# State updates of a gated linear attention as three fp32r products instead of one fp32 product

## The chip, the cores and the metric

The kernel runs on one core of a Trainium2 chip. The core has a matrix engine (PE, with its weight loads shown apart as PEld), a vector engine (DVE), a scalar engine (ACT), a third elementwise engine (POOL) and a queue that issues the transfers (SP). Each engine works through its own queue in order; semaphores make one engine wait for another. The metric is the device time of one execution in microseconds (us), the median of several runs. The scratch memory that all engines use is SBUF; PE writes its products to PSUM, from where DVE and ACT read them. POOL doesn't read PSUM here.

## The reference, cut to what matters

```python
h = rmsnorm(x, norm_g)
q, k, v, z_a, lr_f, lr_b, b_gate, c_gate, h_c, z_c = split(h @ w_in)      # 1024 tokens, 4 heads
# per head and direction (forward, and backward on the flipped sequence), in chunks:
#   o     = att(q, k) @ v  +  q_in @ state
#   state = decay * state  +  k_out.T @ v          # the state update: 128 x 256 per head
o = o_fwd + o_bwd
o = o * rsqrt(mean(o * o) + EPS) * gla_norm_g      # over the 256 columns of a head
y = concat([o * silu(z_a), short_conv(...) * silu(z_c)])
out = rmsnorm(x + y @ w_out, final_g)
```

All inputs and outputs are float32.

## The kernel before, in words

Sequence and feature sizes are 1024; tokens go in 8 blocks of 128 (`t`), there are 4 heads (`h`), keys have 128 and values 256 columns. The first 577 us project `x` to `q`, `k`, `v`, the gates and the convolution, with every fp32 operand split in two fp32r parts (`split`, L151: `hi` is a rounded copy, `lo` the rest) and three products for one, `hi*hi`, `hi*lo`, `lo*hi`; the results go to DRAM by head.

The last stage, which the change touches, runs the heads. For each head `load_head` and `load_z` (L703, L722) bring back decays `b`, keys, queries, values and the gate `z`. Ahead of head 0 its backward states are built in 7 steps. Then, for head h and block t (the loop at L923):

- `output` (L814) adds up to three fp32 products in the PSUM tile `po`: backward state, forward state, and `at` times `v` (L824). ACT squares `po` and sums the squares (`osq`, `oss`, L828), `inv_rms` adds eps on DVE (L147) and raises to -1/2 on POOL (L148), ACT scales `po` by that to `on` (L830). `po` has one buffer.
- `turns` (L856) transposes up to two key blocks on PE (`pk`, L861) and copies each to SBUF on ACT (`ks`, L862): the forward key block of this head and the backward one of the next head, whose states are built one head ahead. `states` (L865) multiplies each with its block of `v` in one fp32 product (`pu`, L869), and DVE adds the product to the decayed state (`s0`, `s1`, L876). In heads 0 to 2 there are two such updates in 7 of the 8 blocks, in head 3 one, in the 7 steps ahead of head 0 one.
- `scores` (L802) makes three fp32 products in `pa`; DVE copies the first to `at` (L809) and overwrites it under two masks (L810, L811). `at` is an operand of the next block's `po`.
- `store` (L833) transposes `on` to `py` on PE, and DVE multiplies it with `z` (`yt`, L844).
- `prep_f` and `prep_b` (L764, L754) compute the decayed queries and keys of the blocks ahead: `dd`, `qs`, `qx`, `kx`, `ko`, `e` on DVE and ACT, `kt` times `k` on POOL (L779). These DVE instructions read two SBUF operands.
- `more` (L887) fills PE between these steps with products of the output projection (`out`, L667), whose results DVE adds to `res` (L669).

In this stage the code fixes only what depends on what; a scheduler of the library, with durations of its own, sets the order of each engine's queue when the kernel is built, and puts in the waits. Another set of instructions can so change the order of all others.

Of the kernel before, what the change touches and what calls it, by code (L numbers as in the profile page):

```python
# [9 lines left out]
F32 = mybir.dt.float32  # L10
F32R = mybir.dt.float32r
I32 = mybir.dt.int32
BF16 = mybir.dt.bfloat16
AF = mybir.ActivationFunctionType
ALU = mybir.AluOpType
# [3 lines left out]
P = 128  # L19
S = 1024  # L20
D = 1024
NH = 4
DK = 128
DV = 256
# [3 lines left out]
EPS = 1e-6  # L28
# [9 lines left out]
def tile_hybrid_gla_shortconv(ctx, tc, x, norm_g, w_in, w_gk_f, b_gk_f, w_gk_b, b_gk_b,  # L38
                              gla_norm_g, conv_w, conv_b, w_out, final_g, out):
    nc = tc.nc  # L40
    V, A, G, T = nc.vector, nc.scalar, nc.gpsimd, nc.tensor
# [6 lines left out]
    stat = ctx.enter_context(tc.tile_pool(name="stat", bufs=4))  # L48
# [15 lines left out]
    z_dram = [dram.tile([P, 2, S], F32, name=f"z_dram{h}") for h in range(NH)]  # L64
# [35 lines left out]
    for d, wg in enumerate((w_gk_f, w_gk_b)):  # L100
        for r in range(4):
            o = d * 64 + r * RANK
# [7 lines left out]
    mhalf = const.tile([P, 1], F32, name="mhalf")  # L110
# [33 lines left out]
    def inv_rms(ss, eps_n):  # L144

        rs = stat.tile([P, 1], F32, name="rs", bufs=6)
        V.tensor_scalar(rs, ss, eps_n, None, ALU.add)  # L147
        G.tensor_tensor(rs, rs, mhalf, ALU.pow)  # L148
        return rs

    def split(hi, lo, src, e_hi=A, e_lo=G):  # L151

        (e_hi.copy if e_hi is A else e_hi.tensor_copy)(hi, src)  # L153
        e_lo.tensor_tensor(lo, src, hi.bitcast(F32), ALU.subtract)  # L154
# [14 lines left out]
    def scale_of(t):  # L169
        sq = xp.tile([P, D], BF16, name="sq", bufs=2)  # L170
        ss = stat.tile([P, 1], F32, name="ss")
        A.activation(sq, xts[t], AF.Square, accum_out=ss)
        return inv_rms(ss, D * EPS)
# [59 lines left out]
    with tc.manual_schedule():  # L233
# [24 lines left out]
        for t in range(NT):  # L258
            ps = bank()[:, 0:DV]
            mul_v(ps, t, wv, 0)  # L260
            if t + 2 < NT:
                rs = scale_of(t + 2)
# [24 lines left out]
    for half in range(2):  # L287
        lps = bank()
        for c in range(ND):
            for j in range(2):  # L290
                T.matmul(lps, lrw[:, c, :], hb[c // 4][half][j][:, c % 4, :],  # L291
                         start=c == 0 and j == 0, stop=c == ND - 1 and j == 1)
# [341 lines left out]
    dq = gl.enter_context(tc.tile_pool(name="dq", bufs=2, reuse_waits="tile"))  # L634
    hd = gl.enter_context(tc.tile_pool(name="hd", bufs=2, reuse_waits="tile"))
    hx = gl.enter_context(tc.tile_pool(name="hx", bufs=2, reuse_waits="tile"))
    pg = gl.enter_context(tc.tile_pool(name="pg", bufs=1, space=PSUM, reuse_waits="tile"))
    GS = 2
# [81 lines left out]
        return r  # L720

    def load_z(h, r):  # L722
        for half in range(2):
            z = hx.tile([P, 2, 512], F32, name="z", bufs=3)
            nc.sync.dma_start(z, z_dram[h][:, :, half * 512:half * 512 + 512])
            r["sz"].append(z)

    def decays(r):
# [73 lines left out]
    def scores(r, g, t):  # L802
        i = t % GS
        pa = pg.tile([P, 3, P], F32, name="pa", bufs=2)
        T.matmul(pa[:, 0], fl(r["kx"][:, t]), fl(g["qx"][:, i]), start=True, stop=True)
        T.matmul(pa[:, 1], fl(g["kt"][0][:, i]), fl(g["qt"][0][:, i]), start=True, stop=True)
        T.matmul(pa[:, 2], fl(g["kt"][1][:, i]), fl(g["qt"][1][:, i]), start=True, stop=True)
        at = dq.tile([P, P], F32, name="at")
        V.tensor_copy(at, pa[:, 0])  # L809
        V.copy_predicated(at, mask_f_i, pa[:, 1])  # L810
        V.copy_predicated(at, mask_b_i, pa[:, 2])  # L811
        return at

    def output(r, g, t, at, s_f):  # L814
        i = t % GS
        o = pg.tile([P, DV], F32, name="po")
        mm = []
        if r["sb"][t] is not None:
            mm.append((fl(g["qs"][1][:, i]), r["sb"][t]))
        if s_f is not None:  # L820
            mm.append((fl(g["qs"][0][:, i]), s_f))
        mm.append((at, r["v"][:, t]))
        for j, (l, m) in enumerate(mm):
            T.matmul(o, l, m, start=j == 0, stop=j == len(mm) - 1)  # L824

        sq = dq.tile([P, DV], BF16, name="osq", bufs=1)
        ss = stat.tile([P, 1], F32, name="oss")
        A.activation(sq, o, AF.Square, accum_out=ss)  # L828
        on = dq.tile([P, DV], F32, name="on")
        A.activation(on, o, AF.Copy, scale=inv_rms(ss, DV * EPS * DK))  # L830
        return on

    def store(h, r, py, t, on):  # L833
        i = t % GS
        if i == 0:
            py[0] = pg.tile([P, 2, GS * P], F32, name="py")
        for e2 in range(2):
            T.transpose(py[0][:, e2, i * P:(i + 1) * P], on[:, e2 * P:(e2 + 1) * P], ident)
        if i == GS - 1:
            r0 = t + 1 - GS  # L840
            yt = dq.tile([P, 2, GS * P], F32, name="yt")
            for e2 in range(2):
                o4 = r0 % 4 * P
                V.scalar_tensor_tensor(yt[:, e2], py[0][:, e2], gng_h[:, e2:e2 + 1],  # L844
                                       r["sz"][r0 // 4][:, e2, o4:o4 + GS * P], ALU.mult, ALU.mult)
            if h < NH - 1:
                nc.sync.dma_start(ya_dram[:, h * 2:h * 2 + 2, r0 * P:(r0 + GS) * P], yt)
                return
            for j in range(GS):
                raw = ws.tile([P, 4, P], F32, name="s", bufs=3)  # L850
                nc.sync.dma_start(raw[:, 0:2], ya_dram[:, 2 * h - 2:2 * h, (r0 + j) * P:(r0 + j + 1) * P])
                y = y_last[r0 + j] = y_pair()
                for k, src in ((0, raw[:, 0:2]), (2, yt[:, :, j * P:(j + 1) * P])):
                    split(y[0][:, k:k + 2], y[1][:, k:k + 2], src)

    def turns(items):  # L856

        pk = pg.tile([P, 2, P], F32, name="pk")
        ks = dq.tile([P, 2, P], F32, name="ks")
        for r, t, d, kt in items:  # L860
            T.transpose(pk[:, d], kt, ident)  # L861
            A.copy(ks[:, d], pk[:, d])  # L862
        return ks

    def states(items, ks, s_f):  # L865

        pu = pg.tile([P, 2, DV], F32, name="pu")
        for r, t, d, kt in items:
            T.matmul(pu[:, d], ks[:, d], r["v"][:, t], start=True, stop=True)  # L869
        for r, t, d, kt in items:  # L870
            s = st.tile([P, DV], F32, name=f"s{d}", bufs=(2, NT + 1)[d])
            old = s_f if d == 0 else r["sb"][t]
            if old is None:
                V.tensor_copy(s, pu[:, d])
            else:
                V.scalar_tensor_tensor(s, old, r["dp"][d][:, t:t + 1], pu[:, d], ALU.mult, ALU.add)  # L876
            if d == 0:
                s_f = s
            else:
                r["sb"][t - 1] = s  # L880
        return s_f
# [23 lines left out]
    for t in range(NT - 1, 0, -1):  # L905
        if t % GS == GS - 1:
            ko1[0, t // GS] = prep_b(heads[0], t + 1 - GS)
        items = [(heads[0], t, 1, fl(ko1[0, t // GS][:, t % GS]))]
        ks = turns(items)
        more(3)  # L910
        states(items, ks, None)
        more(3)
        if t == 4:
            load_z(0, heads[0])
    gs = {(0, 0): {}}
    for _ in prep_f(heads[0], 0, gs[0, 0]):
        pass
    at = {(0, 0): scores(heads[0], gs[0, 0], 0)}
    heads.append(start_head(1))
    ons = []  # L920
    py = [None]
    ahead = iter(())
    for h in range(NH):  # L923
        r = heads[h]
        nxt = heads[h + 1] if h + 1 < NH else None
        s_f = None
        if nxt is not None:
            load_z(h + 1, nxt)
        for t in range(NT):
            n = h * NT + t  # L930
# [14 lines left out]
            def step(k=2):  # L945
                more(share.pop(0))
                for _ in range(k):
                    next(ahead, None)
            g = gs[h, t // GS]
            on = output(r, g, t, at[h, t], s_f)  # L950
            step()
            items = []
# [3 lines left out]
            if nxt is not None and tb > 0:  # L956
                items.append((nxt, tb, 1, fl(ko1[h + 1, tb // GS][:, tb % GS])))
            ks = turns(items) if items else None
            if ons:
                store(*ons.pop())  # L960
            step()
            step(0)
            if items:
                s_f = states(items, ks, s_f)
            step(0 if t % 2 == 0 else 4)
            ons.append((h, r, py, t, on))
            if n + 1 < NH * NT:
                hh, tt = divmod(n + 1, NT)
                if t % GS == GS - 1:
                    for _ in ahead:  # L970
                        pass
                at[hh, tt] = scores(heads[hh], gs[hh, tt // GS], tt)
            step(0)
        if h + 2 < NH:
            heads.append(start_head(h + 2))
    store(*ons.pop())
    more(NT * NT)
    gl.close()
# [22 lines left out]
```

## Time and profile before

| | |
|---|---|
| median of 3 runs | 878.18 us (878.04 to 878.6) |
| the profiled execution | 879.14 us, of which the span from first to last instruction is 877.4 |
| PE busy | 859.9 us, 98% of the span |
| DVE, ACT, POOL busy | 644.3, 374.1, 396.2 us |
| last stage, heads and output projection | from about 577 us to the end |
| fp32 products of state updates | 56, two records each |

How it is read: a busy engine is one that has an instruction under way. PE's products overlap, each starts before the one ahead of it has drained, so their cost is the step from one start to the next and not their length. A chain of waits is read from a timeline: what an instruction waited for stands behind it in brackets, with the idle time.

### The profile page before, as it was taken

How to read it: one execution, taken by the hardware profiler on the slowest of the kernel's cores; microseconds unless marked ns; L12 is line 12 of the kernel's file. 1: busy time of each engine (PE TensorE's matmuls, PEld its weight loads, DVE VectorE, ACT ScalarE, POOL GpSimd, SP SyncE). 2: the span in 40 equal slices, each digit the busy share in tenths (PEclk: the TensorE clock that was granted, in tenths of full speed). 3: DMA queues.
4: the chain of work that ended last, by engine and by line, in shares of the span. 5: the costliest groups of instructions: out<-in, count | busy, mean ns of one | idle time of the engine just before them, and what ended most of it. 6: DMA issues, size and time to landing. Idle time of an engine off the chain costs nothing.

```text
span 877.4 us, 12286 instructions
## 1 busy us (share of the span) xinstructions
PE 859.9 (98%) x4236; PEld 713.9 (81%) x4236; DVE 644.3 (73%) x1181; ACT 374.1 (43%) x771; POOL 396.2 (45%) x349
## 2 busy tenths in 40 slices
PE   7999999999999999999999999999999999999996
PEld 6999987878787877878788888887877787878885
DVE  5889738696868787786864445468799989976664
ACT  4633223354434343544532233334464546542553
POOL 3423756667666666767654453601112122221231
PEclk9999999999999999999999999999999999999999
DMA  8511441314222222413153342579575333310122
GB/s 305 117 55 48 123 120 49 96 52 116 58 87 72 72 85 61 121 48 118 44 163 97 98 127 88 174 238 397 166 231 186 121 126 125 110 37 24 43 79 96
DMA packets 102160, 100.30 MB, mean 114 GB/s; under 512 B 10705, under 2 KB 82385, under 8 KB 101586
## 3 DMA queue, kind: packets, MB, share of 16 engines
q1 hardware_dynamic: 102098, 99.53, 36.3%
q8 instruction: 33, 0.54, 0.3%
q14 instruction: 29, 0.24, 0.1%
HBM read 71.20 MB, written 28.31 MB: 113 GB/s over the span
## 4 chain that ended last, share of the span: by engine, by line
PE 90%; DVE 5%; DMA 3%; issue 1%; ACT 1%; SPq 0%; POOLq 0%; POOL 0%; DVEq 0%; ACTq 0%
PE pb L390 18%; PE pc L390 18%; PE pa L390 18%; PE out L667 16%; PE out L223 5%; PE po L824 3%; PE pu L869 2%; PE pc L466 2%; PE pb L466 2%; PE pa L466 1%; PE out L538 1%; DMA b<-b_dram 1%; DMA k<-k_dram 1%; PE out L291 1%; DMA xt<-in_x 1%
## 5 line engine op out<-in xcount | busy, mean ns | idle before, releaser
L154 POOL TENSOR_TENSOR a_lo<-raw,a_hi 128x512 fp32r<-128x512 f32 x84 | 124.7, 1493 | 43.2 <-ACT a_hi L153 38.7
L154 POOL TENSOR_TENSOR a_lo<-tmp,a_hi 128x512 fp32r<-128x512 f32 x48 | 72.4, 1509 | 101.9 <-ACT a_hi L153 100.3
L153 ACT CAST a_hi<-tmp 128x512 fp32r<-128x512 f32 x48 | 29.6, 617 | 156.4 <-DVE tmp L416 127.7
L153 ACT CAST a_hi<-raw 128x512 fp32r<-128x512 f32 x108 | 65.6, 619 | 64.2 <-POOL a_lo L154 21.1
L148 POOL TENSOR_TENSOR rs<-rs,mhalf 128x1 f32<-128x1 f32 x48 | 28.7, 598 | 142.2 <-DVE rs L147 134.8
L667 PE MATMUL out<-a_hi,y_hi 128*128 128x512 f32 x192 | 88.8, 463 | 0.5 <-ACT y_hi L153 0.5
L154 POOL TENSOR_TENSOR a_lo<-s,a_hi 128x512 fp32r<-128x512 f32 x50 | 74.4, 1488 | 18.8 <-ACT a_hi L153 16.4
L667 PE MATMUL out<-a_hi,y_lo 128*128 128x512 f32 x192 | 76.9, 401 | 0.0
L667 PE MATMUL out<-a_lo,y_hi 128*128 128x512 f32 x192 | 76.7, 400 | 0.0
L779 POOL TENSOR_TENSOR kt<-kt,k 128x256 f32<-128x256 f32 x32 | 26.3, 823 | 95.1 <-ACT kt L776 71.8
L416 DVE TENSOR_TENSOR s<-raw 128x512 f32<-128x512 f32 x24 | 29.1, 1214 | 50.2 <-DMA raw<-in_w_in 49.8
L390 PE MATMUL pc<-h_hi,a_lo 128*128 128x512 f32 x128 | 50.4, 394 | 0.0
L390 PE MATMUL pb<-h_hi,a_lo 128*128 128x512 f32 x128 | 50.4, 393 | 0.0
L390 PE MATMUL pa<-h_hi,a_lo 128*128 128x512 f32 x128 | 50.4, 393 | 0.0
L390 PE MATMUL pa<-h_lo,a_hi 128*128 128x512 f32 x128 | 50.2, 393 | 0.0
L390 PE MATMUL pb<-h_lo,a_hi 128*128 128x512 f32 x128 | 50.2, 393 | 0.0
L390 PE MATMUL pc<-h_lo,a_hi 128*128 128x512 f32 x128 | 50.2, 392 | 0.0
L390 PE MATMUL pb<-h_hi,a_hi 128*128 128x512 f32 x128 | 50.1, 392 | 0.0
L390 PE MATMUL pc<-h_hi,a_hi 128*128 128x512 f32 x128 | 50.1, 392 | 0.0
L390 PE MATMUL pa<-h_hi,a_hi 128*128 128x512 f32 x128 | 50.0, 391 | 0.0
L438 DVE TENSOR_TENSOR tmp<-pa,tmp 128x512 f32<-128x512 f32 x48 | 32.5, 685 | 22.7 <-PE pa L390 22.1
L438 DVE TENSOR_TENSOR tmp<-pc,tmp 128x512 f32<-128x512 f32 x48 | 32.5, 686 | 20.0 <-PE pc L390 19.5
(263 smaller groups left out, 2514.1 us busy)
## 6 DMA issues: line engine op xcount, KB each, us to landing
raw<-in_w_in SPq DMA_DIRECT2D x56, 512.0 KB, 4.1
raw<-in_w_out SPq DMA_DIRECT2D x16, 512.0 KB, 4.0
xt<-in_x SPq DMA_DIRECT2D x8, 512.0 KB, 8.4
yc_dram<-tmp SPq DMA_DIRECT2D x16, 256.0 KB, 3.3
b_dram<-u SPq DMA_DIRECT2D x8, 512.0 KB, 2.6
z_dram<-tmp SPq DMA_DIRECT2D x16, 256.0 KB, 2.9
s<-yc_dram SPq DMA_DIRECT2D x16, 256.0 KB, 4.2
raw<-in_x SPq DMA_DIRECT2D x8, 512.0 KB, 6.1
```

Source lines behind the costliest of these rows:

```text
L148: G.tensor_tensor(rs, rs, mhalf, ALU.pow)
L153: (e_hi.copy if e_hi is A else e_hi.tensor_copy)(hi, src)
L154: e_lo.tensor_tensor(lo, src, hi.bitcast(F32), ALU.subtract)
L223: last_mm[0] = T.matmul(ps, h_tile(a, c, t), wv[c // 4][w_][:, c % 4, :], start=part == 0 and c == 0, stop=part == 2 and c == ND - 1)
L390: T.matmul(ps, a[x0][:, k], b_[x1][:, k], start=start and k == 0 and j == 0, stop=stop and k == n - 1 and j == 2, skip_group_check=not start)
L416: V.tensor_tensor(f, x0, x1, op)
L438: step(V.tensor_tensor(f, ps, x, ALU.add))
L466: T.matmul(ps[:, t * DV:(t + 1) * DV], b_[x1][:, k, tok], fl(o[k // 2][x0])[:, k % 2 * DV:k % 2 * DV + DV], start=k == 0 and j == 0, stop= ...
L667: T.matmul(ps, a[:, j, :], w, start=j == 0 and i == 0, stop=j == 3 and i == 2)
L779: G.tensor_tensor(kk, kk, k4, ALU.mult)
L824: T.matmul(o, l, m, start=j == 0, stop=j == len(mm) - 1)
L869: T.matmul(pu[:, d], ks[:, d], r["v"][:, t], start=True, stop=True)
```

## The change

The state update's fp32 product becomes three fp32r products of split parts. `turns` now splits `v` of each update in `vh` (a copy on ACT) and `vl` (a subtraction on POOL), and the key block in `ks` (ACT's copy out of PSUM, now rounded to fp32r) and `kl` (a subtraction on DVE, one instruction over both key blocks of a step). `states` multiplies `ks*vh`, `ks*vl`, `kl*vh`. Three other edits: the first copy of `at` moves from DVE to ACT; `po` becomes one fixed PSUM tile of 257 columns, the last of which holds the square root of the eps term, so that the sum of squares includes eps and `inv_rms` falls away in `output` (POOL's power reads `oss` directly); `z` is loaded in four pieces of 256 columns with five buffers instead of two of 512 with three.

```diff
     def load_z(h, r):
-        for half in range(2):
-            z = hx.tile([P, 2, 512], F32, name="z", bufs=3)
-            nc.sync.dma_start(z, z_dram[h][:, :, half * 512:half * 512 + 512])
+        n = GS * P
+        for i in range(S // n):
+            z = hx.tile([P, 2, n], F32, name="z", bufs=5)
+            nc.sync.dma_start(z, z_dram[h][:, :, i * n:i * n + n])
             r["sz"].append(z)
...
         at = dq.tile([P, P], F32, name="at")
-        V.tensor_copy(at, pa[:, 0])
+        A.copy(at, pa[:, 0])
         V.copy_predicated(at, mask_f_i, pa[:, 1])
...
+    po = pg.tile([P, DV + 1], F32, name="po")
+    V.memset(po[:, DV:DV + 1], (DV * EPS * DK) ** 0.5)
     def output(r, g, t, at, s_f):
-        o = pg.tile([P, DV], F32, name="po")
+        o = po[:, 0:DV]
...
-        A.activation(sq, o, AF.Square, accum_out=ss)
+        A.activation(sq, po, AF.Square, accum_out=ss)
+        rs = stat.tile([P, 1], F32, name="rs", bufs=6)
+        G.tensor_tensor(rs, ss, mhalf, ALU.pow)
         on = dq.tile([P, DV], F32, name="on")
-        A.activation(on, o, AF.Copy, scale=inv_rms(ss, DV * EPS * DK))
+        A.activation(on, o, AF.Copy, scale=rs)
...
     def turns(items):
+        vs = []
+        for r, t, d, kt in items:
+            v = tuple(dq.tile([P, DV], F32R, name=n, bufs=b) for n, b in (("vh", 3), ("vl", 2)))
+            split(*v, r["v"][:, t])
+            vs.append(v)
         pk = pg.tile([P, 2, P], F32, name="pk")
-        ks = dq.tile([P, 2, P], F32, name="ks")
+        ks, kl = (dq.tile([P, 2, P], F32R, name=n) for n in ("ks", "kl"))
         for r, t, d, kt in items:
             T.transpose(pk[:, d], kt, ident)
             A.copy(ks[:, d], pk[:, d])
-        return ks
+        ds = [d for r, t, d, kt in items]
+        both = slice(min(ds), max(ds) + 1)
+        V.tensor_tensor(kl[:, both], pk[:, both], ks[:, both].bitcast(F32), ALU.subtract)
+        return ks, kl, vs
-    def states(items, ks, s_f):
+    def states(items, kv, s_f):
+        kh, kl, vs = kv
         pu = pg.tile([P, 2, DV], F32, name="pu")
-        for r, t, d, kt in items:
-            T.matmul(pu[:, d], ks[:, d], r["v"][:, t], start=True, stop=True)
+        for (r, t, d, kt), (vh, vl) in zip(items, vs):
+            for j, (a, v) in enumerate(((kh, vh), (kh, vl), (kl, vh))):
+                T.matmul(pu[:, d], a[:, d], v, start=j == 0, stop=j == 2)
```

The change also gives the scheduler another set of instructions. Three places of the built programs follow, all in head 1 around the output of its fifth block; numbers in names are buffers of the build, L numbers those of the respective file.

PE before, behind the last product of `po` (its first key transpose stands ahead of that product): one transpose, six projection products, the two updates.

```order
L861 MATMUL pk_6767<-ident_148,ko1_6740 128x128
L667 MATMUL out_6722<-a_hi_6082,y_hi_6718 128x512
L667 MATMUL out_6722<-a_lo_6083,y_hi_6718 128x512
L667 MATMUL out_6722<-a_hi_6082,y_lo_6719 128x512
L667 MATMUL out_6722<-w_hi_6092,y_hi_6718 128x512
L667 MATMUL out_6722<-w_lo_6093,y_hi_6718 128x512
L667 MATMUL out_6722<-w_hi_6092,y_lo_6719 128x512
L869 MATMUL pu_6796<-v_5763,ks_6768 128x256
L869 MATMUL pu_6796<-v_6415,ks_6768 128x256
```

PE now, behind the last product of `po`, up to the first product that reads `kl`:

```order
L873 MATMUL pk_6973<-ident_148,ko0_6897 128x128
L845 MATMUL py_6888<-ident_148,on_6862 128x128 x2
L667 MATMUL out_6922<-a_hi_6196,y_hi_6918 128x512
L667 MATMUL out_6922<-a_lo_6197,y_hi_6918 128x512
L667 MATMUL out_6922<-a_hi_6196,y_lo_6919 128x512
L873 MATMUL pk_6973<-ident_148,ko1_6940 128x128
L667 MATMUL out_6922<-w_hi_6206,y_hi_6918 128x512
L667 MATMUL out_6922<-w_lo_6207,y_hi_6918 128x512
L667 MATMUL out_6922<-w_hi_6206,y_lo_6919 128x512
L886 MATMUL pu_7004<-vh_6965,ks_6974 128x256
L886 MATMUL pu_7004<-vl_6966,ks_6974 128x256
L886 MATMUL pu_7004<-vh_6965,kl_6975 128x256
```

Both key transposes and those of `on` now stand behind `po`, and the second key transpose has three projection products, not six, between it and the updates.

ACT before, at the same place: both key copies stand ahead of `on`.

```order
L862 COPY ks_6768<-pk_6767 128x128
L828 ACTIVATE osq_6748,oss_6749<-po_6744 128x256
L862 COPY ks_6768<-pk_6767 128x128
L830 ACTIVATE on_6751<-po_6744,rs_6752 128x256
L733 ACTIVATE dc0_7037<-b0_7033 128x16
```

ACT now:

```order
L833 ACTIVATE osq_6947,oss_6948<-po_5335 128x257
L874 CAST ks_6974<-pk_6973 128x128
L734 ACTIVATE dc0_7271<-b0_7267 128x16
L837 ACTIVATE on_6952<-po_5335,rs_6950 128x256
L874 CAST ks_6974<-pk_6973 128x128
L153 CAST vh_7052<-v_6563 128x256
L153 CAST vh_7141<-v_5825 128x256
```

The second key copy has moved behind `on`, and the copies of `v` for later blocks have come in behind it.

DVE before, in the same block, from the state updates to the end of `at`:

```order
L876 SCALAR_TENSOR_TENSOR s0_6799<-s0_6712,dp0_5771,pu_6796 128x256
L876 SCALAR_TENSOR_TENSOR s1_6801<-s1_6714,dp1_6427,pu_6796 128x256
L786 TENSOR_TENSOR qx_6908<-q_6419,e_6917 128x2x64
L786 TENSOR_TENSOR qx_6908<-q_6419,e_6983 128x2x64
L809 COPY at_6811<-pa_6807 128x128
L778 TENSOR_TENSOR qt0_6911<-qt0_6911,q_6419 128x256
L810 COPY_PREDICATED at_6811<-mask_f_160,pa_6807 128x128
L772 TENSOR_TENSOR dd_6938<-b1_6411 128x256
L811 COPY_PREDICATED at_6811<-mask_b_161,pa_6807 128x128
```

DVE now:

```order
L893 SCALAR_TENSOR_TENSOR s0_7011<-s0_6912,dp0_5833,pu_7004 128x256
L893 SCALAR_TENSOR_TENSOR s1_7013<-s1_6914,dp1_6575,pu_7004 128x256
L787 TENSOR_TENSOR qx_7130<-q_6567,e_7139 128x2x64
L787 TENSOR_TENSOR qx_7130<-q_6567,e_7217 128x2x64
L779 TENSOR_TENSOR qt0_7133<-qt0_7133,q_6567 128x256
L811 COPY_PREDICATED at_7023<-mask_f_160,pa_7019 128x128
L773 TENSOR_TENSOR dd_7170<-b1_6559 128x256
L812 COPY_PREDICATED at_7023<-mask_b_161,pa_7019 128x128
```

The copy is gone from this queue and the rest stands as it stood.

## Rows read from the trace of the kernel before

**Rows 1.** The page: busy us of each engine, share of span, instructions.
```profile
PE 859.9 (98%) x4236; PEld 713.9 (81%) x4236; DVE 644.3 (73%) x1181; ACT 374.1 (43%) x771; POOL 396.2 (45%) x349
```

**Rows 2.** Stretches of heads 0, 1, 2: length, each engine's busy us (instructions), clock, DMA.
```profile
626.50:675.40 48.90, 47.11 (x243) 38.62 (x242) 46.04 (x143) 28.36 (x84) 11.44 (x16) 1.00 0.58 188
675.40:725.40 50.00, 48.75 (x248) 39.25 (x247) 45.19 (x144) 23.86 (x76) 11.06 (x16) 1.00 0.39 127
725.40:774.90 49.50, 48.68 (x246) 39.39 (x246) 46.70 (x140) 27.56 (x81) 11.85 (x16) 1.00 0.34 104
```

**Rows 3.** Waits, 577 us to the end: who waited for whom, us, times, longest.
```profile
PEld po L824 <- DVE at L811: 9.0, 18, 1.1
...
PE po L824 <- DVE at L811: 3.0, 9, 0.8
```

**Rows 4.** Timeline, fp32 products of 128x256: start, us, engine, line, operands, records.
```profile
705.53 1.03 PE L824 MATMUL po<-s,qs 128*128 128x256 f32 x4
706.39 0.27 PE L861 MATMUL pk<-ident,ko 128*128 128x128 f32 x1
```

**Rows 5.** Timeline of PE in an earlier stage, fp32r products of 128x256, 28 rows.
```profile
83.74 0.28 PE L466 MATMUL pc<-a_hi,t_lo 128*128 128x256 f32 x1
83.86 0.28 PE L466 MATMUL pc<-a_lo,t_hi 128*128 128x256 f32 x1
...
86.92 0.28 PE L466 MATMUL pa<-a_hi,t_lo 128*128 128x256 f32 x1
```

**Rows 6.** DVE's groups from 577 us: busy us, mean ns, idle before, releaser.
```profile
L876 DVE SCALAR_TENSOR_TENSOR s<-s,dp,pu 128x256 f32<-128x256 f32 x48 | 21.3, 474 | 4.5 <-PE pu L869 4.3
L772 DVE TENSOR_TENSOR dd<-b 128x256 f32<-128x256 f32 x32 | 16.0, 502 | 0.1
...
L787 DVE TENSOR_TENSOR qs<-qx,dc 128x128 f32<-128x128 f32 x32 | 12.0, 375 | 0.0
...
L809 DVE COPY at<-pa 128x128 f32<-128x128 f32 x32 | 9.1, 285 | 1.3 <-PE pa L807 1.2
...
L147 DVE TENSOR_SCALAR rs<-oss 128x1 f32<-128x1 f32 x32 | 4.8, 149 | 7.3 <-ACT osq L828 6.8
```

**Rows 7.** Timeline, POOL's product beside DVE; the last row is undisturbed.
```profile
705.66 0.73 POOL L779 TENSOR_TENSOR kt<-kt,k 128x256 f32<-128x256 f32 x1 [3.00 <-ACT kt L776]
705.80 0.88 DVE L772 TENSOR_TENSOR dd<-b 128x256 f32<-128x256 f32 x1
...
706.93 0.70 PE L824 MATMUL po<-v,at 128*128 128x256 f32 x2 [0.27 <-DVE at L811]
...
709.21 0.41 DVE L772 TENSOR_TENSOR dd<-b 128x256 f32<-128x256 f32 x1
```

**Rows 8.** Issues by tile: count, KB each, median us from issue to landing.
```profile
v<-v_dram SPq DMA_DIRECT2D x4, 1024.0 KB, 6.6
z<-z_dram SPq DMA_DIRECT2D x8, 512.0 KB, 5.7
```

**Rows 9.** Timeline, head 1, behind its fifth block's output.
```profile
700.56 0.70 PE L824 MATMUL po<-v,at 128*128 128x256 f32 x2
...
701.58 0.19 ACT L828 ACTIVATION_READ_ACCUMULATOR osq<-po 128x1 f32 x1
...
701.88 0.15 DVE L147 TENSOR_SCALAR rs<-oss 128x1 f32<-128x1 f32 x1 [0.34 <-ACT osq L828]
...
702.11 0.55 POOL L148 TENSOR_TENSOR rs<-rs,mhalf 128x1 f32<-128x1 f32 x1 [5.33 <-DVE rs L147]
...
702.60 1.02 PE L869 MATMUL pu<-v,ks 128*128 128x256 f32 x4
702.69 0.47 ACT L830 ACTIVATE on<-po,rs 128x256 f32<-128x256 f32 x1 [0.76 <-POOL rs L148]
```

**Rows 10.** Timeline, head 2: a key copy behind `on`; POOL beside a state update.
```profile
758.48 0.47 ACT L830 ACTIVATE on<-po,rs 128x256 f32<-128x256 f32 x1 [0.73 <-POOL rs L148]
...
758.85 0.26 ACT L862 COPY ks<-pk 128x128 f32<-128x128 f32 x1
...
759.16 0.70 PE L869 MATMUL pu<-v,ks 128*128 128x256 f32 x2 [0.33 <-ACT ks L862]
...
759.55 0.75 POOL L779 TENSOR_TENSOR kt<-kt,k 128x256 f32<-128x256 f32 x1 [1.11 <-issue]
...
759.90 0.87 DVE L876 SCALAR_TENSOR_TENSOR s<-s,dp,pu 128x256 f32<-128x256 f32 x2 [0.18 <-PE pu L869]
```

More of the change, by code (lines that the diff above doesn't have):

```diff
@@ L824, in output @@
             T.matmul(o, l, m, start=j == 0, stop=j == len(mm) - 1)
-        sq = dq.tile([P, DV], BF16, name="osq", bufs=1)
+        sq = dq.tile([P, DV + 1], BF16, name="osq", bufs=1)
         ss = stat.tile([P, 1], F32, name="oss")
-        A.activation(sq, o, AF.Square, accum_out=ss)
+        A.activation(sq, po, AF.Square, accum_out=ss)
+        rs = stat.tile([P, 1], F32, name="rs", bufs=6)
+        G.tensor_tensor(rs, ss, mhalf, ALU.pow)
         on = dq.tile([P, DV], F32, name="on")
-        A.activation(on, o, AF.Copy, scale=inv_rms(ss, DV * EPS * DK))
+        A.activation(on, o, AF.Copy, scale=rs)
         return on
@@ L842, in store @@
             for e2 in range(2):
-                o4 = r0 % 4 * P
                 V.scalar_tensor_tensor(yt[:, e2], py[0][:, e2], gng_h[:, e2:e2 + 1],
-                                       r["sz"][r0 // 4][:, e2, o4:o4 + GS * P], ALU.mult, ALU.mult)
+                                       r["sz"][r0 // GS][:, e2], ALU.mult, ALU.mult)
             if h < NH - 1:
```

## Prediction

> **What bounds the kernel now.** I read the page first: TensorE is busy 98% of the span [rows 1]; what remains is the stages. The change touches only the last one, from 577 us on, where the four attention heads run between the products of the output projection. By stretch [rows 2], PE is busy 97 to 98% while heads 0, 1 and 2 run (626.5 to 774.9), and DVE is nearly as full there: 137.9 of 148.4 us, 10.5 us left. ACT has half its time free and POOL three quarters. So two engines are close to the bound, PE sets the time, and what PE loses are waits inside a block of 128 tokens (24 blocks in that stretch, 6.2 us each). The list of waits names the largest: the last product of `po` waits for `at`, which DVE finishes: 3.0 us seen as idle PE and 9.0 us seen by the weight load ahead of it [rows 3]. Spacing the products' ends, I put the real loss at some 7.6 us of the stage's 300. The reader should keep two questions apart: how many product slots PE must issue, and which chain ends last ahead of the products that wait.
>
> **Product slots.** Each key block's update is one fp32 product of 128x256, recorded as two instructions. Four such records stand 0.86 us apart from what follows them (705.53 to 706.39) [rows 4], so one product takes 0.43 us. The three new products are fp32r of 128x256: 27 steps from 83.74 to 86.92 [rows 5] make 0.118 us each, 0.353 for three. There are 56 updates (7 ahead of the heads, 7 times 2 in each of heads 0 to 2, 7 in head 3): 56 x (0.43 - 0.353) = **-4.4 us** of PE time. The weights change at each of these rows too, so the price holds for products with new weights.
>
> The Trainium skill (TensorE: Matmul & The Clock Gate, Back-to-back issue gap) gives 256 columns N/2.4 + 2.5 ns, which is 109 ns; the rows above show 118, and the measurement decides. By the page's figure the term would be -5.8 us, an estimate.
>
> **Work beside the products, on DVE.** Per block the copy of `at` (0.285) and the eps addition (0.149) go [rows 6], 32 of each: -13.9. The subtraction for `kl` comes, 21 times over both halves (0.474, as the state update, which also reads 128x256 from PSUM) and 14 times over one (0.285): +13.9. DVE's own load is even. ACT gets 56 copies of `v` (128x256) and 32 of `at`, some 1.1 us per block, into its free half; POOL gets 56 subtractions of 0.73 us (its 128x256 product with `k` [rows 7]), some 1.5 us per block, into its free three quarters. The z loads become four of 256 KB instead of two of 512 KB per head: on SP's queue each waits for the same kind of release as before (an earlier z tile read by DVE), the weights and stores behind it stand a few positions earlier or later, and none of them is among the waits of the trace; I cost it at nothing, and at most at one landing of 5.7 us [rows 8] if a tile were late. The eps column adds one element to a 0.38 us square.
>
> **The new wait ahead of the third product.** Before, the second key copy was all that the second update needed. Now `kl` covers both halves, so the third product needs pk's second transpose, ACT's copy of it and DVE's subtraction. The order (first two fences) shows what is new: in 10 of the 21 blocks with two updates ACT's second key copy stands behind `on`, which waits for POOL's power, which waits for the square of `po`. At the place shown, today [rows 9]: `po` ends at 701.26, the square with its read-out at 701.77, the eps addition hands over at 702.03, POOL starts at 702.11, `on` at 702.69. Without the addition the 0.34 us from 701.77 to 702.11 shrink to about 0.1, so `on` starts at 702.45; the next ACT instruction starts 0.37 later (758.48 to 758.85) [rows 10], the copy takes 0.26, the subtraction 0.47, hand-overs 0.1: `kl` at 703.65, which is 2.4 us behind the end of `po`; 2.7 where an exponential stands between. PE meanwhile issues, at that place, two transposes for pk and two for py (0.11 each), six projection products (0.23, twice the columns of [rows 5]) and two updates' products: 2.05 us, from 701.11 on (702.60 less the 1.49 that lie between today). It arrives at 703.16 and waits 0.5. By the same count the cover is 2.05 at two of the ten places (0.5 each), 2.28 at five (three with an exponential between, 0.57 each, two at 0.26) and 2.51 at three (0.34, and twice nothing): **+3.6 us**. The trace has this pattern once today, and it does cost: the second update waits 0.33 for ACT's copy behind `on` [rows 10]; that place goes, so **+3.3**. Bounds: 0 if PE is late at these places anyway, and +6 if the weight load adds 0.1 to 0.2 at each and DVE's queue ahead of `kl` (up to 2.4 us of work at three of them) ends later than ACT's.
>
> **The wait for `at`.** Three things move. DVE's queue between the state update and the second predicated copy loses the copy, 0.23 us of its time. ACT's copy now comes between, 0.26 and a hand-over, but DVE reaches the predicated copy later than that by the order shown (third pair of fences). And PE arrives earlier at about half the places, by 0.11 to 0.33, because transposes have moved behind `po`. Against this stands what [rows 7] show: while POOL multiplies `kt` (705.66, 0.73 us), DVE's `dd`, two SBUF inputs, takes 0.88 instead of 0.41 (709.21), its end follows POOL's, and `po` waits 0.27 for `at` right behind it. A state update, which reads PSUM, keeps its 0.87 for two beside the same POOL instruction (759.55, 759.90) [rows 10]. The first `vl` of a block runs beside such PSUM work, the second ends about 0.3 us after DVE turned to SBUF work ahead of `at`. I take -0.23 - 0.1 (removed addition) + 0.3 as **0**; bounds -3.8 (half of the 7.6) and +6 (0.3 at 20 places).
>
> The Trainium skill states the same as a rule (SBUF — State Buffer, Who interferes with whom): a DVE instruction with two SBUF inputs and a GpSimd instruction that reads SBUF exclude each other for the whole instruction. The trace agrees for `dd`, 0.88 against 0.41. It speaks against this change, which adds 56 such GpSimd instructions; it is the second rival.
>
> **Sum.** -4.4 + 3.3 + 0 = -1.1 us. On the profiled execution: 879.14 (span 877.4 and 1.7 around it) becomes 878.0; the median of the runs lies 0.96 below the profiled one, so **877.1 us**, a ratio of 0.9988.
>
> **Rivals.** *The waits for `at` halve and the new wait is small:* a shorter DVE queue lets `at` come in time, -3.8, and PE being early at `kl` is worth only +1: -4.4 - 3.8 + 1 = -7.2, and half-way between this and the forecast -4; 871 to 874. For it: the copy and the addition leave the fuller engine. Against it: the second `vl` takes their place. *POOL's subtractions bind DVE, slower:* 42 `vl` in heads 0 to 2 block SBUF work of DVE; from 10.5 / 42 = 0.25 us each DVE, not PE, sets the block's length there. At 0.36, between that and the 0.47 of `dd`, it is 15.1 - 10.5 = +4.6, and PE's saved slots are worth nothing: 882.8; at 0.47, +9.2: 887. For it: `dd` in [rows 7], and the means of `dd` (502) and `qs` (375) in [rows 6], which lie 90 ns above undisturbed ones over all 32, though only one `kt` a block runs. Against it: at least the first `vl` falls beside PSUM work. *The three products don't save:* should fp32r with a wait on every second one space at 0.144 or more instead of 0.118, the term is zero and the waits remain: +3.3, 881.5; the rows of 128x256 show no such spacing, but they stand in one long run without waits.
>
> **How the numbers follow.** Forecast 0.50, its own range 875 to 880; first rival 0.20; second 0.22; third 0.08. A difference under 0.2% (1.8 us) can't be told from no change. The forecast's centre lies within that; of its 0.50 I put 0.20 beyond it on the fast side and 0.02 on the slow one. Faster 0.20 + 0.20 = 0.40; same 0.28 + 0.03 of the third rival = 0.31; slower 0.02 + 0.22 + 0.05 = 0.29. The range leaves out the far end of the first rival (some 0.07) and the upper part of the second (some 0.10): 872 to 883.
>
> **What would show it.** In the profile after: updates of three records spaced 0.118; PE waits for `kl` from DVE at about ten places, 0.1 to 0.6 each, with ACT's key copy behind `on`; waits of `po` for `at` of 6 to 9 us in sum, as now; DVE's busy time in the stage up by 10 to 13 us though its instructions weigh the same, all of it on instructions with two SBUF inputs. Wrong if PE waits for `vl` (POOL late) or ACT waits at `vh` for a load of `v` (6.6 us from issue to landing) [rows 8], which no wait of the trace names today; or if PE is never early at `kl`.

## The result, and the profile after

The changed kernel takes 887.67 us (887.07 to 888.84) against 878.39 beside it: a ratio of 1.0099, 95% interval 1.0085 to 1.0112. I had forecast 877.1; it is slower by 1.0%. Runs on other chips are compared below by their ratios to the kernel before, 0.001 being 0.88 us. Times are medians; the views of a run come from one execution, which lay 6.2 us above the run's median for e4, 3.3 for e8 and 2.1 for e12.

The page of the changed kernel, busy us of each engine and the chain that ended last, answers to [rows 1]; the last line is the chain of the kernel before:

```profile
PE 861.1 (97%) x4292; PEld 711.5 (80%) x4292; DVE 654.8 (74%) x1153; ACT 397.6 (45%) x859; POOL 438.1 (49%) x405
...
PE 79%; DVE 12%; DMA 3%; ACT 3%; POOL 1%; issue 1%; SPq 0%; POOLq 0%; ACTq 0%
```

```profile
PE 90%; DVE 5%; DMA 3%; issue 1%; ACT 1%; SPq 0%; POOLq 0%; POOL 0%; DVEq 0%; ACTq 0%
```

DVE's share of the chain was 5% and is 12%. The stretches of heads 0, 1 and 2 of the changed kernel, in the columns of [rows 2] (length; busy us and instructions of PE, PEld, DVE, ACT, POOL; clock; DMA):

```profile
627.83:680.53 52.70, 47.23 (x259) 38.32 (x258) 46.97 (x132) 32.70 (x102) 21.43 (x29) 1.00 0.55 178
680.53:732.31 51.78, 49.47 (x263) 39.05 (x262) 48.59 (x140) 31.35 (x102) 21.52 (x30) 1.00 0.40 128
732.31:783.05 50.74, 48.38 (x260) 38.92 (x259) 46.75 (x128) 33.10 (x102) 23.23 (x31) 1.00 0.32 100
sum 155.22, PE 145.08 PEld 116.29 DVE 142.31 ACT 97.15 POOL 66.17; mean PE 48.36 PEld 38.76 DVE 47.44 ACT 32.38 POOL 22.06
```

6.8 of the 8.7 us by which the span grew lie here (148.4 to 155.2), and DVE is busy 4.4 us longer (137.9 to 142.3). The granted clock is full in these stretches (1.00).

To see what PE lost I took every product of the last stage and its step from the end of the product ahead. The median step of its kind is its slot; what goes over it by more than 60 ns is a stall. Before: 275.6 us of slots and 11.8 of stalls. After: 270.7 and 24.8. So the slots fell by 4.9 (4.4 at the updates, as meant; the rest is 1 ns in the median step of 768 products of `out`), and the stalls grew by 13.0, of which 8.3 stand at the updates (`pu`, 0.6 to 8.9), 2.4 at `pk`, 1.3 at `out`, 1.0 at `po`.

The list of waits of the changed kernel, last stage (who waited for whom, us, times, longest), PE and its weight loads, answers to [rows 3]:

```profile
PEld po L830 <- DVE at L812: 9.9, 19, 1.2
...
PEld pk L873 <- ACT ks L874: 7.2, 15, 2.9
...
PEld pu L886 <- DVE kl L877: 6.0, 11, 0.8
...
PE po L830 <- DVE at L812: 4.5, 9, 0.9
...
PE pu L886 <- DVE kl L877: 2.3, 7, 0.4
```

The timeline of the changed kernel at one update in head 1 (start, us, engine, line, operands, in brackets the idle time and its cause):

```profile
689.28 0.39 PE L886 MATMUL pu<-vh,kl 128*128 128x256 f32 x1 [0.26 <-DVE kl L877]
...
689.50 0.28 PE L886 MATMUL pu<-vh,ks 128*128 128x256 f32 x1
...
689.62 0.28 PE L886 MATMUL pu<-vl,ks 128*128 128x256 f32 x1
...
689.67 1.49 POOL L154 TENSOR_TENSOR vl<-v,vh 128x256 fp32r<-128x256 f32 x2
...
689.74 0.82 DVE L788 TENSOR_TENSOR qs<-qx,dc 128x128 f32<-128x128 f32 x1
689.74 0.28 PE L886 MATMUL pu<-vh,kl 128*128 128x256 f32 x1
```

The second update's three products end 0.12 apart, as in [rows 5]. The first update's third product waits for `kl`. And beside POOL's two `vl`, a `qs` of DVE takes 0.82 us.

One place in head 0 costs 2.7 us by itself. On ScalarE the small exponential `dc` waits for a load of `b`; the square, the key copy and with them PE's next transpose stand behind it (timeline of the changed kernel):

```profile
661.14 0.23 ACT L734 ACTIVATE dc<-b 128x16 f32<-128x16 f32 x1 [3.66 <-DMA b<-b_dram]
...
661.93 0.25 ACT L874 CAST ks<-pk 128x128 fp32r<-128x128 f32 x1
...
662.24 0.33 PE L873 MATMUL pk<-ident,ko 128*128 128x128 f32 x1 [2.47 <-ACT ks L874]
```

In the kernel before, this block's square and key copy stood ahead of the same `dc` in ScalarE's queue, so its wait held up neither:

```profile
657.43 0.37 ACT L828 ACTIVATE osq<-po 128x256 bf16<-128x256 f32 x1
...
657.79 0.26 ACT L862 COPY ks<-pk 128x128 f32<-128x128 f32 x1
...
662.83 0.23 ACT L733 ACTIVATE dc<-b 128x16 f32<-128x16 f32 x1 [2.34 <-DMA b<-b_dram]
```

The two loads of `b` for this head are now issued together at 652.87, before at 650.35 and 655.11. The one that `dc` waits for isn't later for it: it landed at 662.81 before and lands at 661.05, counted from the head's first `osq` 36.3 us and 33.2. What moved is the place of `dc`.

So there were three suspects: the wait for `kl` (A), POOL's subtractions `vl`, which hold up DVE (B), and the other order of the queues that came with the change (C).

### The profile page after: what moved, and what is told of

It is laid out like the page before. It is cut to its first block, busy times and chain, and to the rows that moved or that the text cites. A ratio compares the mean times of both kernels' runs of the same rounds, so it can differ in the third digit from the quotient of the medians.

```text
span 886.1 us, 12520 instructions
## 1 busy us (share of the span) xinstructions
PE 861.1 (97%) x4292; PEld 711.5 (80%) x4292; DVE 654.8 (74%) x1153; ACT 397.6 (45%) x859; POOL 438.1 (49%) x405
## 4 chain that ended last, share of the span: by engine, by line
PE 79%; DVE 12%; DMA 3%; ACT 3%; POOL 1%; issue 1%; SPq 0%; POOLq 0%; ACTq 0%
PE pb L390 17%; PE pc L390 17%; PE pa L390 17%; PE out L667 10%; PE out L223 5%; PE po L830 2%; PE pb L466 2%; PE pc L466 2%; DMA b<-b_dram 2%; DVE res L669 1%; PE pa L466 1%; PE pu L886 1%; DVE dd L773 1%; PE out L538 1%; DVE qt L779 1%
## 5 line engine op out<-in xcount | busy, mean ns | idle before, releaser
L154 POOL TENSOR_TENSOR a_lo<-raw,a_hi 128x512 fp32r<-128x512 f32 x84 | 124.3, 1488 | 43.6 <-ACT a_hi L153 39.8
L154 POOL TENSOR_TENSOR a_lo<-tmp,a_hi 128x512 fp32r<-128x512 f32 x48 | 72.4, 1508 | 101.8 <-ACT a_hi L153 100.3
L667 PE MATMUL out<-a_hi,y_hi 128*128 128x512 f32 x192 | 82.9, 432 | 0.3 <-ACT y_hi L153 0.3
L154 POOL TENSOR_TENSOR a_lo<-s,a_hi 128x512 fp32r<-128x512 f32 x50 | 73.8, 1476 | 19.0 <-ACT a_hi L153 16.5
L154 POOL TENSOR_TENSOR vl<-v,vh 128x256 fp32r<-128x256 f32 x56 | 43.5, 782 | 66.0 <-ACT vh L153 32.8
L835 POOL TENSOR_TENSOR rs<-oss,mhalf 128x1 f32<-128x1 f32 x32 | 19.6, 612 | 69.4 <-ACT osq L833 69.3
L153 ACT CAST a_hi<-s 128x512 fp32r<-128x512 f32 x50 | 30.9, 619 | 37.9 <-PE pa L390 10.4
```

The costliest lines, as they stand in the source:

```text
L667: T.matmul(ps, a[:, j, :], w, start=j == 0 and i == 0, stop=j == 3 and i == 2)
L835: G.tensor_tensor(rs, ss, mhalf, ALU.pow)
```

## Experiments

**Which part brings the loss?** In e1 the products are undone; in e2 they are done alone, with the z pieces, and `po` is again one tile of 256 columns per output.

```diff
# e1_rest: the changed kernel without vh, vl and kl, and
-            for j, (a, v) in enumerate(((kh, vh), (kh, vl), (kl, vh))):
-                T.matmul(pu[:, d], a[:, d], v, start=j == 0, stop=j == 2)
+            T.matmul(pu[:, d], ks[:, d], r["v"][:, t], start=True, stop=True)
# e2_products: the changed kernel, but
-        A.copy(at, pa[:, 0])
+        V.tensor_copy(at, pa[:, 0])
...
-        A.activation(sq, po, AF.Square, accum_out=ss)
...
+        A.activation(sq, o, AF.Square, accum_out=ss)
...
-        A.activation(on, o, AF.Copy, scale=rs)
+        A.activation(on, o, AF.Copy, scale=inv_rms(ss, DV * EPS * DK))
```

> The changed kernel with its state updates as one fp32 product again (no vh, vl, kl; the key copy in fp32); the copy of at on ScalarE, the eps column and the z pieces stay. Theory A (the split products bring the loss: 9 us net of the 4.8 us of slots that they save): this kernel loses the new waits, gives up the 4.8, and DVE has 13.9 us less to do than before: 874 to 879. Theory C (the other order of the queues that comes with the small edits, the two adjacent loads of b above all, brings the loss): 881 to 884.

> The kernel before with the three products of split parts, and the z pieces, without which they find no room; the copy of at stays on DVE and eps stays an addition. Theory A: the whole loss is here, and DVE is 13.9 us fuller than in the changed kernel: 888 to 893. Theory C: the loss comes with the copy of at and the eps column, so 877 to 882 here.

Measured: e1 881.43 (ratio 1.0023, 1.0011 to 1.0035), e2 886.11 (1.0084, 1.0067 to 1.0101). The products bring most of it (7.4 us), but the small edits cost 2.0 although they took 4.8 us of work from DVE in heads 0 to 2. e1 lies in the range of C, e2 in neither. A single cause doesn't do.

**kl and vl, each away.** The products stay, reading the rounded part in place of the missing low part.

```diff
# e3_no_kl: the changed kernel, but
...
-        V.tensor_tensor(kl[:, both], pk[:, both], ks[:, both].bitcast(F32), ALU.subtract)
-        return ks, kl, vs
+        return ks, ks, vs
# e4_no_vl: the changed kernel, but
...
-            split(*v, r["v"][:, t])
...
+            A.copy(vh, r["v"][:, t])
...
# e5_no_vl_no_kl: both
```

> The changed kernel without the subtraction for kl; the third product of each update reads ks again (the low part of the key is left out), so PE has the same slots. Theory A (PE is early at the third product, 5.7 us of stalls in 12 places, as the trace spaces them): these go, and DVE has 14 us less to do: 878 to 882. Theory B (POOL's subtractions hold up DVE, which is what sets the length of the blocks): the collisions stay; only what DVE gains by the missing instructions shows, 883 to 886.

> The changed kernel without the subtraction for vl; the second product reads vh again (the low part of v is left out), so PE has the same slots and POOL 56 instructions less. Theory A: only the waits for vl themselves go, 1.3 us: 885 to 887. Theory B: the 8 us by which DVE's instructions are longer beside these subtractions go, and with them most of the loss: 878 to 881.

> The changed kernel without both subtractions: all three products read the rounded parts vh and ks (both low parts are left out), PE has the same slots. Without kl alone nothing was won, without vl alone 8 us. Theory B (POOL's subtractions make DVE late; the wait for kl is only the place where that shows, and without kl it shows at the next one, the wait for at): with both gone the 5 us of pu stalls that were left without vl go too, 873 to 877. Theory D (kl costs nothing by itself, and only vl counts): as without vl alone, 879 to 881.

Measured: e3 887.84 (1.0103, 1.0088 to 1.0118), e4 879.87 (1.0011, 0.9989 to 1.0033), e5 876.99 (0.9975, 0.9965 to 0.9986). Without `vl` 7.7 us go (0.0088), as B expects. Without both, e5 lies at the upper end of B's range. Without `kl` alone nothing goes, and e3 lies above both of its ranges: stalls at `pu` fall from 8.9 to 3.7, those at `po` rise from 8.6 to 15.7. I first read that as "`kl` costs nothing by itself"; e8 shows it to be wrong.

**What of vl costs?** In e6 POOL fills the tile with zeros, twice, instead of subtracting: it is busy 0.62 us per update where the subtraction takes 0.78, PE waits for the same tile, but POOL reads nothing. In e7 it subtracts twice.

```diff
# e6_vl_memset: the changed kernel, but
...
-            split(*v, r["v"][:, t])
...
+            A.copy(vh, r["v"][:, t])
+            for _ in range(2):
+                G.memset(vl.bitcast(F32), 0.0)
# e7_vl_twice: the changed kernel, and
+            G.tensor_tensor(v[1], r["v"][:, t], v[0].bitcast(F32), ALU.subtract)
```

> The changed kernel with each subtraction for vl replaced by two fills of the same tile with zeros on POOL (the low part of v is left out): POOL is occupied for some 0.6 us per update and PE still waits for vl, but POOL reads nothing from SBUF. Theory B1 (the loss is the mutual exclusion of DVE's two-input instructions and a POOL instruction that reads SBUF): the time falls to that without vl, 878 to 882. Theory B2 (the loss is that kt and the power, which stand behind vl in POOL's queue, come later): 884 to 888.

> The changed kernel with each subtraction for vl done twice, one behind the other, into the same tile. Theory B: the price doubles, 8 us more, 893 to 899, and DVE's instructions beside L154 are longer by twice as much. Theory E (the one subtraction happens to stand badly in this order, and the price is of the order, not of the amount): 885 to 891.

Measured: e6 881.74 (1.0036, 1.0022 to 1.0051), e7 907.2 (1.0321, 1.0304 to 1.0337). e6 lies in the range of B1, e7 above both of its ranges. The queues of e4, e6 and e7 stand nearly as in the changed kernel (of DVE's 1153 instructions 3 stand elsewhere in e4 and e6, 20 in e7), so this comparison is nearly free of the order. The same place of head 1 as above, timeline of e6:

```profile
685.73 1.30 POOL L870 MEMSET vl<- 128x256 f32 x4
...
685.81 0.28 DVE L788 TENSOR_TENSOR qs<-qx,dc 128x128 f32<-128x128 f32 x1
```

`qs` takes 0.28 beside the fills, 0.82 beside the subtractions. Over the whole stage, each DVE instruction against the median of its kind with nothing of POOL beside it (one that meets two POOL instructions is counted to the first): 110 instructions beside e6's fills are 0.16 us longer in sum; in the changed kernel 144 beside subtractions of L154 (56 `vl` and 16 others) are 9.2 us longer, against 0.8 in the kernel before, which has the 16 alone. Heads 0 to 2, sums of the stretches, of e4, e6 and e7 in this order:

```profile
sum 152.23, PE 144.87 PEld 117.77 DVE 138.14 ACT 97.14 POOL 35.55; mean PE 48.29 PEld 39.26 DVE 46.05 ACT 32.38 POOL 11.85
```
```profile
sum 151.55, PE 143.81 PEld 116.53 DVE 139.07 ACT 96.85 POOL 59.67; mean PE 47.94 PEld 38.84 DVE 46.36 ACT 32.28 POOL 19.89
```
```profile
sum 169.21, PE 147.65 PEld 116.40 DVE 157.84 ACT 97.18 POOL 101.13; mean PE 49.22 PEld 38.80 DVE 52.61 ACT 32.39 POOL 33.71
```

POOL is busy 59.7 us in e6 and 66.2 in the changed kernel, and the time falls by 5.5 us (0.0063): so most of it is the reading, not the occupation. PE's stalls fall with it from 24.8 to 18.2: 3.8 of that at the updates, where `kl` comes late, 1.2 at `po`, 0.8 at `pk`, 0.7 at `out`. The drop at `pk` is that of one place, the load of `b` (2.7 against 1.6), where kernels of one order differ by as much. The other 2.2 of `vl`'s 7.7 can be POOL's queue; this is a rough bound, as the fills are a fifth shorter and e4's interval is 0.0022 to either side. In e7 DVE is busy 15.5 us longer again, and the time rises by 19.5: the second dose, 0.35 us per `vl`, costs more than twice the first (0.14).

The Trainium skill (SBUF — State Buffer, Who interferes with whom) says that a DVE instruction with two SBUF inputs contends with a GpSimd instruction that reads SBUF and not with one that only writes it. e6 agrees: 0.28 against 0.82.

**The same orders.** Of DVE's instructions 139 in e1 and 128 in e3 stand elsewhere in its queue than in the changed kernel, besides the 35 that are removed, so the scheduler's other order may hide or feign a price. In e8 and e9 edges that fix the issue order alone hold each queue of the last stage in the changed kernel's order, by a table taken from its build.

```diff
# e8_no_kl_same_order: e3, e9_fp32_same_order: e1, each with
     gl = ExitStack()
+    start = len(tc.nc.cur_bb.bb.instructions)
...
+    pin(tc, start)
```

> Again the changed kernel without the subtraction for kl (the low part of the key is left out, the third product reads ks), but with every engine's queue of the last stage held in the order of the changed kernel, which the scheduler had rearranged on DVE and ScalarE in the run before. Theory F (what DVE gains by the missing 35 instructions, 7.6 us in heads 0 to 2, it loses again because POOL's subtractions then stand beside its two-input SBUF work): again less than 2 us, 885 to 888. Theory G (the rearranged order hid the gain): the stalls at the third product go, 880 to 883.

> The changed kernel with its updates as one fp32 product (no vh, vl, kl), every queue of the last stage held in the order of the changed kernel, the fp32 product standing where the first of the three stood. It pays the late load of b, 2.7 us, as the changed kernel does. If the loss lies in the split products themselves (theory B): 879 to 882, since e1 in its own order gave 881.4 and an order made for other work should cost a little but not bring the collisions. If it lies in the order that came with the change (theory C): 884 to 888.

Measured: e8 883.02 (1.0044, 1.003 to 1.0058), e9 876.9 (0.9976, 0.9964 to 0.9988). In one order `kl` costs 4.8 us (0.0055), at the upper edge of theory G's range; the order of e3 had hidden it. DVE's sum in heads 0 to 2 falls by 4.9 of the 7.6 us that `kl` takes there; over the stage, DVE's instructions beside `vl` are 9.0 us longer in sum in e8 and 7.6 in the changed kernel, which is a part of the difference. And e9, the same instructions as e1, is 4.1 us faster than e1 (0.0047) and 2.1 below both of its ranges: the order that came with the change is a good one for the fp32 products. Theory C falls: in one order the split products cost 10.8 us (0.0123). Waits of PE in e9, last stage:

```profile
PEld pk L894 <- ACT ks L895: 5.7, 15, 1.3
PEld po L856 <- DVE at L838: 4.9, 12, 1.4
PE po L856 <- DVE at L838: 1.9, 3, 1.1
```

Its stalls are 8.6 us, the fewest of all kernels, and those at `po` 4.1.

**The load of b.**

```diff
# e11_dc_late: the changed kernel, and
+            if t == 2 and nxt is not None:
+                with tc.issue_after(last_sq[0].ins):
+                    decays(nxt, 0)
```

> The changed kernel with the small exponential of the second b tile (dc of direction 0, which is not needed for a head yet) queued on ScalarE behind the third block's square, so that ScalarE's queue no longer waits for that tile's load at the start of a head. If the 2.69 us wait of pk behind that load is lost time: 884 to 886. If other work of the block would have waited there anyway: 887 to 888.

Measured 884.65 (1.0066, 1.0051 to 1.0081): 2.9 us, as the first case expects. Its queues differ elsewhere too (77 of DVE's instructions), and by spacing the stalls at `pk` fell by 1.7 only (5.1 to 3.4), so I put the load's share at 1.7 to 2.9 us; that is an estimate.

**What a slot is worth.** e12 is e5 and e13 is e10, in the changed kernel's order.

```diff
# e10_one_product: the changed kernel without kl and vl, and
-            for j, (a, v) in enumerate(((kh, vh), (kh, vl), (kl, vh))):
-                T.matmul(pu[:, d], a[:, d], v, start=j == 0, stop=j == 2)
+            T.matmul(pu[:, d], kh[:, d], vh, start=True, stop=True)
# e12_no_vl_no_kl_same_order: e5, e13_one_product_same_order: e10, each with
+    pin(tc, start)
# e14_fp32_dc_late_same_order: e1 with e11's edit, in e11's order
```

> The changed kernel with one fp32r product of the rounded parts per update (both low parts and their two products are left out): PE has 112 products of 0.118 us less than the kernel without vl and kl, 13.2 us. Theory H (PE sets the length, so slots count in full): 877.0 less 13.2, 864. Theory I (in heads 0 to 2 DVE sets it, 132 us busy and 14 us of hand-overs): slots count only in the lead-in and head 3, 14 of 56 updates, 3.3 us: 873 to 875.

> The changed kernel without both subtractions (both low parts are left out, the three products read vh and ks), every queue of the last stage held in the order of the changed kernel. Against e9, which differs by one fp32 product for three and by the copies of v on ScalarE, this shows what the three products are worth by themselves when nothing of DVE and POOL hangs on them: 4.4 us less, 872 to 873.5, if PE's slots count in full there; 876 to 878 if they don't.

> The same with one product of the rounded parts instead of three (both low parts and their products are left out): 13.2 us of slots less than e12. Theory H (PE sets the length): 859 to 861. Theory I (DVE sets it in heads 0 to 2): 868 to 871, as e10 gave with an order of its own.

> One fp32 product per update, the small edits of the change, dc of direction 0 queued late as in e11, every queue of the last stage in the order of e11: the exact kernel that the runs point to. e9 paid 1.07 us where pk waits behind the load of b; without it 875.5 to 876.5. If e11's order is worse for it than that of the changed kernel: 877 to 880.

Measured: e10 868.94 (0.9892, 0.9862 to 0.9922), e12 875.01 (0.9946, 0.9925 to 0.9968), e13 868.03 (0.9869, 0.9852 to 0.9887), e14 876.78 (0.9972, 0.9954 to 0.9991).

e10, in its own order, lies between its two cases. e12 against e9: three products save 2.6 us (0.0030) where 4.4 of slots go; the intervals of the two overlap a little, and it lies between its two cases. In the profiled executions e12 loses 2.0 us more at the load of `b` (3.1 against 1.1), but e12's is above its median by 2.1 and e9's below by 1.4, so this doesn't explain the medians. e13 against e12: 13.2 us of slots are worth 6.8 (0.0077), at the lower edge of theory I: stalls at `po` for `at` rise from 5.1 to 10.6. Heads 0 to 2 of e12 and e13:

```profile
sum 147.61, PE 142.27 PEld 118.04 DVE 130.94 ACT 96.19 POOL 35.58; mean PE 47.42 PEld 39.35 DVE 43.65 ACT 32.06 POOL 11.86
```
```profile
sum 141.29, PE 134.73 PEld 106.32 DVE 129.25 ACT 94.64 POOL 34.60; mean PE 44.91 PEld 35.44 DVE 43.08 ACT 31.55 POOL 11.53
```

There e13 needs 6.3 us less, 1.6 of it at the load of `b` (3.1 against 1.6), where 42 of the 56 updates would give 9.9: PE is now ahead of DVE's `at` more often.

e9 and e14 compute what the kernel before does, in fp32, and are faster than both kernels, by 2.1 and 2.5 us. e14 lies between its two cases. They can't be told from each other, so putting `dc` off brings the fp32 kernel nothing that shows. e10 and e13 are faster still, but they leave out both low parts and so compute something coarser.

## Why the prediction was wrong

In ratios, all in the changed kernel's order: kernel before to e9, -2.1 us (small edits and the order); e9 to e12, -2.6 (three products for one); e12 to the changed kernel, +13.4 (`kl` and `vl` together: 8.6 for `vl` and 4.8 for `kl` on top of it, or 5.7 for `kl` and 7.7 for `vl` on top). By construction that makes the 8.7 measured.

- **Product slots, -4.4: right.** By spacing 4.4 at the updates (the rounded numbers of the sum give 4.3; and PE was busy 96% in head 0, where I wrote 97 to 98). What of it shows in the time when nothing hangs on the products is 2.6; why not all of it isn't shown.
- **DVE's own load even: right.** In heads 0 to 2 the copy of `at` and the eps addition took 7.7 us, `kl` takes 7.6. But the rise to 142.3 comes from longer instructions, which I had forecast only as a sign, at 10 to 13 us for the stage, and put into no term of the sum; DVE's busy time from 577 us on rose by 9.7 (236.3 to 246.0).
- **The wait for `kl`, +3.3: right in mechanism, too small.** 4.8 in one order (5.7 without `vl`), within the bounds of 0 and 6. The list of waits names `kl` at 7 products and 11 weight loads where I counted 10 places: in some it is the first of a block's two updates that waits, as at 689.28.
- **The wait for `at`, 0: this is the step that failed.** The wait itself grew by 1.0 only. What failed is that I let `vl` act there alone, charged it 0.3 us at a place and set that off against DVE's shorter queue, so that it came to nothing; `vl` cost 7.7 us of the kernel's time (e4), and 5.5 of them go when POOL only stops reading (e6). Without `vl` and its reads the stalls at `po` do fall, from 7.6 to 4.8 (e4) or 4.1 (e9), though to 7.4 only in e6: what the first rival hoped for is there, and with `vl` they are 8.6. And most of `vl`'s price is elsewhere: of the stalls that its reads bring, 3.8 us are at the updates and 1.2 at `po`. By stretch, between e6 and the changed kernel, 2.3 us lie ahead of the first head (the stage's first projection product to the first `osq`: 41.8 against 44.1), where I had counted none of the seven updates, 3.7 in heads 0 to 2, 0.7 behind them.
- **The second rival named the cause, with the wrong price.** It let DVE take over only when all its 10.5 us of idle time were filled, from 0.25 us per `vl`. `vl` made DVE busy 4.2 us longer in heads 0 to 2 (138.1 in e4 to 142.3), 0.10 each, and that was enough; the changed kernel still has 12.9 us of DVE idle there. Its 887 at 0.47 each is near the measured time by luck: it stands for 19.7 us of longer DVE instructions in these heads. The idle time is not room that has to fill up first: where an instruction is late ahead of `kl`, `s` or `at`, PE can be late at once. The lead-in shows it (timeline of the changed kernel, at 600 us):

```profile
599.79 1.53 POOL L154 TENSOR_TENSOR vl<-v,vh 128x256 fp32r<-128x256 f32 x2
...
599.89 0.82 DVE L761 TENSOR_TENSOR ko<-k,e 128x128 f32<-128x128 f32 x1
...
600.64 0.83 DVE L762 TENSOR_TENSOR ko<-kx,dc 128x128 f32<-128x128 f32 x1
...
601.39 0.41 DVE L891 COPY s<-pu 128x256 f32<-128x256 f32 x1
...
601.95 0.36 PE L886 MATMUL pu<-vh,ks 128*128 128x256 f32 x1 [0.65 <-DVE s L891]
```

Two `ko` take 0.82 and 0.83 beside two `vl`, where 0.28 is the median, the state's copy behind them comes late, and PE waits 0.65 for it.

- **The loads, at nothing, at most 5.7.** 1.7 to 2.9, within the bound, but not by `z`: in the new order PE's key copy stands behind a `dc` that waits for `b`. I looked for `z`, the weights and the stores among the waits and left out `b`, for which ScalarE waited 8.1 us at three places before, 4.7 of them ahead of head 0; I had not followed what is queued behind it.
- **The small edits** are worth -2.1 in one order and +2.0 in another with the same instructions. The three pieces of the queues shown ahead of the prediction could not tell that: an order made for another set of instructions is itself worth some 4 us here, as much as the terms that I summed. The copy of `at`, the eps column and the z pieces were never undone one by one.
- **The third rival didn't occur:** the products space at 0.12 (median step 0.118).

Open: which rows of the two orders make e9 faster than e1, how the small edits' share divides, and how much of `vl`'s price is POOL's queue rather than the reads (some 2 us).

## What to carry to other kernels

Here an engine beside the bound one, 93% busy, had no slack to be filled: price what makes its instructions late by the place where they stand, in all parts of the stage, and not by its idle time. Before moving elementwise work to an idle engine, see what the two engines share; a subtraction on a half idle POOL cost 0.14 us of the whole kernel's time each, and with fills in their place 5.5 of the 7.7 us went. And where a scheduler sets the order, compare kernels in one held order before giving a part its price: the first measurement of `kl` was 0 us in its own order and 4.8 in the same.

## What the runs showed of the hardware

POOL's power over 128x1, which also reads SBUF, holds up no DVE instruction here: those beside the powers of the last stage are as long as alone, to within 0.02 us in sum, so the exclusion for a whole instruction, of which the prediction speaks, doesn't hold for it. In the changed kernel at 687 us, a `qx`, a `dd` and a `qs`, each with two SBUF inputs, keep their undisturbed 0.28, 0.41 and 0.28 beside a power of 0.70:

```profile
686.92 0.70 POOL L835 TENSOR_TENSOR rs<-oss,mhalf 128x1 f32<-128x1 f32 x1 [0.40 <-ACT osq L833]
686.93 0.28 DVE L787 TENSOR_TENSOR qx<-q,e 128x128 f32<-128x128 f32 x1
...
687.13 0.41 DVE L773 TENSOR_TENSOR dd<-b 128x256 f32<-128x256 f32 x1
...
687.47 0.28 DVE L788 TENSOR_TENSOR qs<-qx,dc 128x128 f32<-128x128 f32 x1
```

And a short DVE instruction isn't spared: a `dp` of 128x8, 0.16 us by itself, took 0.72 beside one `vl` of 0.73 (changed kernel, timeline):

```profile
708.57 0.73 POOL L154 TENSOR_TENSOR vl<-v,vh 128x256 fp32r<-128x256 f32 x1 [1.01 <-PE pu L886]
708.59 0.72 DVE L736 TENSOR_TENSOR dp<-dc 128x8 f32<-128x8 f32 x1
```
